# Row sums of a 16384 x 1024 matrix: two-part row ownership, an early store, and a last row in three pieces

## The chip, the cores and the metric

The kernel runs on one core of one Trainium2 chip. The metric is the device time of one execution in microseconds (us). A profile's *span* is about 1.8 us shorter than the time of the same execution (for the profiled execution of the kernel before: 164.42 us of time, 162.6 us of span). A *packet* is one piece of a transfer as the trace records it on one of the core's 16 DMA engines. A DMA has *landed* when the last of its completion signals (updates of a semaphore, a counter that instructions wait for) is recorded.

## The reference

```python
x = randn(32, 512, 1024) as float32          # 64 MiB
out = (np.sum(x, axis=-1) / 1024.0).astype(np.float32)     # (32, 512), 64 KiB
```

## The kernel before

Each of the 128 partitions (the rows of the on-chip memory) owns 128 consecutive rows, so its part of the input starts 512 KiB after its neighbour's, and its results are one run of 512 bytes of the output. Blocks of 14 rows come in through three buffers. VectorE sums some rows of a block in one instruction, and ScalarE sums the others one at a time, with the accumulator of its activation. The blocks get smaller towards the end, and the last row comes in two pieces. One store writes all results at the very end.

```python
xr = x.tensor.reshape((P, J, D)).ap()          # P = J = 128, D = 1024
out_v = out.tensor.reshape((P, J)).ap()
# ... (bulk: 8 loads of 14 rows, one of 8; tail: 4 rows, 2 rows)
c = 704
t = one.tile([P, D], F32, name="row")          # last row but one
tc.keep_in_program_order(nc.sync.dma_start(out=t, in_=xr[:, j, :]))
act_sum(part[:, 0:1], t[:, c:])
nc.vector.reduce_sum(out=part[:, 1:2], in_=t[:, :c], axis=AX)
nc.vector.tensor_scalar(out=res[:, j : j + 1], in0=part[:, 1:2], scalar1=part[:, 0:1],
                        scalar2=scale, op0=ADD, op1=MULT)
nc.vector.tensor_scalar_mul(out=res[:, :j], in0=res[:, :j], scalar1=scale)
j += 1
t = one.tile([P, D], F32, name="last")         # last row, two pieces
tc.keep_in_program_order(nc.sync.dma_start(out=t[:, :c], in_=xr[:, j, :c]))
tc.keep_in_program_order(nc.sync.dma_start(out=t[:, c:], in_=xr[:, j, c:]))
act_sum(part[:, 2:3], t[:, :c])
nc.vector.reduce_sum(out=part[:, 3:4], in_=t[:, c:], axis=AX)
nc.vector.tensor_scalar(out=res[:, j : j + 1], in0=part[:, 3:4], scalar1=part[:, 2:3],
                        scalar2=scale, op0=ADD, op1=MULT)
tc.keep_in_program_order(nc.sync.dma_start(out=out_v, in_=res))
```

## Time and profile before

| | before |
|---|---|
| time, median of 3 | 163.96 us (163.89 to 164.11) |
| span of the profiled execution | 162.6 us |
| last byte of the loads is in | 158.90 us |
| store issued | 160.22 us |
| packets of the store | 161.07 to 161.42 us |
| store landed | 161.77 us |
| 57,344-byte packets: median, mean, longest | 2116, 2138, 2967 ns |

The last load byte, the store's packets and the packet durations come from the trace's record of single DMA packets, and the landing from its record of completion signals. The other numbers are lines of the profile.

From the page of the kernel before: busy time by engine, the first line of the chain of waits that ended last, and the store's entry among the DMA issues (its last number is us from issue to landing).

```profile
DVE 79.3 (49%) x16; ACT 61.1 (38%) x115; POOL 0.2 (0%) x4
...
DMA 74%; DVE 18%; another core or an unknown queue 5%; SPq 1%; issue 0%; DVEq 0%
...
out_dram<-res SPq DMA_DIRECT2D x1, 64.0 KB, 1.5
```

No engine is busy even half of the time, and three quarters of the chain is DMA. Next, the same kernel by stretches of time; the last two columns are the share of the 16 DMA engines in use and the GB/s that they moved.

```profile
core 0: us, DVE busy (x) ACT busy (x) POOL busy (x), PEclk, DMA share, GB/s
50.00:100.00 50.00, 26.06 (x3) 19.03 (x36) 0.00 (x0) 1.00 0.99 426
100.00:144.00 44.00, 21.67 (x3) 16.92 (x33) 0.00 (x0) 1.00 1.00 433
...
160.00:162.60 2.60, 0.20 (x1) 0.00 (x0) 0.00 (x0) 1.00 0.09 25
```

The DMA engines are full until the loads end. A 57,344-byte packet in 2116 ns is 27.1 GB/s on one engine, or 434 GB/s for sixteen, and that is the speed seen. The engines have no idle time left in these stretches that a reordering could fill, and the median of 2116 ns is the same in the trace of every run of this case. So what follows the last load byte is what is left to shorten. (That nothing could make the packets themselves quicker is argued here, not shown.) The timeline of that end (start, duration, engine, line, operation, output and input):

```profile
start us, us, engine line op out<-in xcount [idle before <-releaser]
...
159.03 0.76 ACT L50 ACTIVATE junk<-last 128x704 f32<-128x704 f32 x1 [0.32 <-DMA last<-in_x_dram]
159.27 0.21 DVE L76 TENSOR_SCALAR res<-part 128x1 f32<-128x1 f32 x1
159.40 0.47 DVE L87 TENSOR_REDUCE part<-last 128x1 f32<-128x320 f32 x1
159.72 0.19 ACT L50 ACTIVATION_READ_ACCUMULATOR junk<-last 128x1 f32 x1
159.98 0.21 DVE L88 TENSOR_SCALAR res<-part 128x1 f32<-128x1 f32 x1
160.22 0.35 SPq L91 DMA_DIRECT2D out_dram<-res  x1
```

The last VectorE sum starts at 159.40, the combine at 159.98, the store's issue at 160.22. After the issue 2.4 us pass until the span ends at 162.65: the store itself and the end of the program. The waits of the queue that issues the DMAs show one delay that costs nothing, and the wait for the store that does:

```profile
engine line waited for: us in total, times, longest us
...
SPq L91 <- DMA t<-in_x_dram: 5.5, 1, 5.5
SPq L122 <- DMA out_dram<-res: 1.0, 1, 1.0
```

The first line is the store waiting for an earlier load, which is over long before its data are ready (L91 is the store). The second is the end of the program (L122) waiting for the store to land.

### The profile page before, as it was taken

What the parts mean: (1) busy time and instruction counts of PE and PEld (TensorE: products, weight loads), DVE (VectorE), ACT (ScalarE), POOL (GpSimd) and SP (SyncE); (2) the same over time, 40 slices, a digit from 0 to 9 for tenths busy, and PEclk for the clock granted to TensorE, in tenths of its full rate; (3) what the DMA queues carried; (4) which work ended last, traced back from release to release, by engine and by line L of the source; (5) the groups of instructions that cost most, each with busy time, mean ns of one, the idle gap of its engine ahead of it and who ended that gap; (6) DMA issues with size and microseconds to landing.
All of it is one profiled execution on the core that took longest, in us unless ns stands there. A gap on an engine that the chain in (4) does not pass through costs nothing.

```text
span 162.6 us, 213 instructions
## 1 busy us (share of the span) xinstructions
DVE 79.3 (49%) x16; ACT 61.1 (38%) x115; POOL 0.2 (0%) x4
## 2 busy tenths in 40 slices
DVE  0000099207940596039801990099108930697893
ACT  3000096006800490029201940095007700692882
POOL 0000000000000000000000000000000000000000
DMA  6999999989999999899999999999999999998990
GB/s 226 451 451 451 451 437 395 437 353 409 451 451 451 451 451 437 381 423 395 423 423 451 451 453 451 451 451 437 409 409 423 409 423 423 443 435 383 423 373 22
DMA packets 2161, 67.18 MB, mean 413 GB/s; under 512 B 240, under 2 KB 496, under 8 KB 752
## 3 DMA queue, kind: packets, MB, share of 16 engines
q1 hardware_dynamic: 2160, 67.18, 96.5%
q14 instruction: 1, 0.01, 0.0%
HBM read 67.11 MB, written 0.07 MB: 413 GB/s over the span
## 4 chain that ended last, share of the span: by engine, by line
DMA 74%; DVE 18%; another core or an unknown queue 5%; SPq 1%; issue 0%; DVEq 0%
DMA t<-in_x_dram 48%; DMA tail<-in_x_dram 25%; DVE res L56 17%; DVE part L75 0%; SPq L61 0%; SPq L66 0%; DVE part L87 0%; DVE res L79 0%; DVE res L88 0%; DVE res L76 0%; DVEq L88 0%; DVEq L76 0%; DVEq L79 0%
## 5 line engine op out<-in xcount | busy, mean ns | idle before, releaser
L56 DVE TENSOR_REDUCE res<-t 128x8 f32<-128x8192 f32 (+1 forms) x9 | 73.9, 8212 | 79.9 <-DMA t<-in_x_dram 79.9
L50 ACT ACTIVATE junk<-t 128x1024 f32<-128x1024 f32 x52 | 52.5, 1009 | 96.7 <-DMA t<-in_x_dram 96.7
L50 ACT ACTIVATION_READ_ACCUMULATOR junk<-t 128x1 f32 x52 | 9.7, 186 | 0.0
L56 DVE TENSOR_REDUCE res<-tail 128x2 f32<-128x2048 f32 (+1 forms) x2 | 3.5, 1753 | 0.7 <-DMA tail<-in_x_dram 0.7
L50 ACT ACTIVATE junk<-tail 128x1024 f32<-128x1024 f32 x3 | 3.1, 1022 | 0.9 <-DMA tail<-in_x_dram 0.9
L50 ACT ACT_TABLE_LOAD x1 | 1.3, 1283 | 0.7 <-PEq L108 0.7
L50 ACT ACTIVATE junk<-last 128x704 f32<-128x704 f32 x1 | 0.8, 761 | 0.3 <-DMA last<-in_x_dram 0.3
L75 DVE TENSOR_REDUCE part<-row 128x1 f32<-128x704 f32 x1 | 0.9, 880 | 0.0
L50 ACT ACTIVATION_READ_ACCUMULATOR junk<-tail 128x1 f32 x3 | 0.6, 186 | 0.0
L50 ACT ACTIVATE junk<-row 128x320 f32<-128x320 f32 x1 | 0.4, 441 | 0.1
L87 DVE TENSOR_REDUCE part<-last 128x1 f32<-128x320 f32 x1 | 0.5, 475 | 0.0
L79 DVE TENSOR_SCALAR res<-res 128x126 f32<-128x126 f32 x1 | 0.2, 228 | 0.1
L88 DVE TENSOR_SCALAR res<-part 128x1 f32<-128x1 f32 x1 | 0.2, 214 | 0.1
L76 DVE TENSOR_SCALAR res<-part 128x1 f32<-128x1 f32 x1 | 0.2, 214 | 0.1
L50 ACT ACTIVATION_READ_ACCUMULATOR junk<-last 128x1 f32 x1 | 0.2, 187 | 0.0
L50 ACT ACTIVATION_READ_ACCUMULATOR junk<-row 128x1 f32 x1 | 0.2, 186 | 0.0
L108 POOL MEMSET const-bfloat16-1.0<- 128x1 bf16 x1 | 0.1, 101 | 0.0
L108 POOL MEMSET const-uint8-127<- 128x1 uint8 x1 | 0.1, 101 | 0.0
L108 POOL MEMSET const-float32-0.0<- 128x1 f32 x1 | 0.1, 98 | 0.2 <-issue 0.2
L108 POOL MEMSET const-float32-1.0<- 128x1 f32 x1 | 0.1, 98 | 0.0
## 6 DMA issues: line engine op xcount, KB each, us to landing
t<-in_x_dram SPq DMA_DIRECT2D x8, 7168.0 KB, 42.1
t<-in_x_dram SPq DMA_DIRECT2D x1, 4096.0 KB, 34.8
tail<-in_x_dram SPq DMA_DIRECT2D x1, 2048.0 KB, 39.3
tail<-in_x_dram SPq DMA_DIRECT2D x1, 1024.0 KB, 41.4
row<-in_x_dram SPq DMA_DIRECT2D x1, 512.0 KB, 42.2
last<-in_x_dram SPq DMA_DIRECT2D x1, 352.0 KB, 42.6
last<-in_x_dram SPq DMA_DIRECT2D x1, 160.0 KB, 42.5
out_dram<-res SPq DMA_DIRECT2D x1, 64.0 KB, 1.5
```

Source lines behind the costliest of these rows:

```text
L50: nc.scalar.activation(junk[:, :n], src, COPY, accum_out=dst)
L56: nc.vector.reduce_sum(out=res[:, j : j + d], in_=t[:, :d, :], axis=AX)
L75: nc.vector.reduce_sum(out=part[:, 1:2], in_=t[:, :c], axis=AX)
L76: nc.vector.tensor_scalar(out=res[:, j : j + 1], in0=part[:, 1:2], scalar1=part[:, 0:1], scalar2=scale, op0=ADD, op1=MULT)
L79: nc.vector.tensor_scalar_mul(out=res[:, :j], in0=res[:, :j], scalar1=scale)
L87: nc.vector.reduce_sum(out=part[:, 3:4], in_=t[:, c:], axis=AX)
L88: nc.vector.tensor_scalar(out=res[:, j : j + 1], in0=part[:, 3:4], scalar1=part[:, 2:3], scalar2=scale, op0=ADD, op1=MULT)
L108: nc = _bacc.Bacc("TRN2", target_bir_lowering=False, num_devices=1)
```

## The change

The intent: nearly all results should leave while the end of the loads is being summed, so that the last store carries little, and the tail after the last load should be short. For this the rows are split in two parts. A partition owns 126 rows of the first part and 2 of the second. The store of the first part goes out as soon as it is summed and scaled. The last row comes in three pieces; the sums of the first two are written beside the third, so that one reduction of 258 columns finishes it. The multiply of the first part moves from VectorE to GpSimd.

```diff
-    xr = x.tensor.reshape((P, J, D)).ap()
-    out_v = out.tensor.reshape((P, J)).ap()
+    L = 2
+    M = J - L
+    x_main = bass.AP(tensor=x.tensor, offset=0, ap=[[M * D, P], [D, M], [1, D]])
+    x_last = bass.AP(tensor=x.tensor, offset=P * M * D, ap=[[L * D, P], [D, L], [1, D]])
+    o_main = bass.AP(tensor=out.tensor, offset=0, ap=[[M, P], [1, M]])
+    o_last = bass.AP(tensor=out.tensor, offset=P * M, ap=[[L, P], [1, L]])
 # ... (cut: the block loads keep their sizes; the row before the last is split at 768, not 704.
#      q and r hold two columns each: q takes VectorE's sums, r those of ScalarE, already scaled.
#      For the last row r is 0, because its ScalarE sum goes into pc)
-    tc.keep_in_program_order(nc.sync.dma_start(out=t[:, :c], in_=xr[:, j, :c]))
-    tc.keep_in_program_order(nc.sync.dma_start(out=t[:, c:], in_=xr[:, j, c:]))
-    act_sum(part[:, 2:3], t[:, :c])
-    nc.vector.reduce_sum(out=part[:, 3:4], in_=t[:, c:], axis=AX)
-    nc.vector.tensor_scalar(
-        out=res[:, j : j + 1], in0=part[:, 3:4], scalar1=part[:, 2:3], scalar2=scale, op0=ADD, op1=MULT
-    )
-    tc.keep_in_program_order(nc.sync.dma_start(out=out_v, in_=res))
+    a, b = 512, 768
+    pa = one.tile([P, a], F32, name="pa")
+    pb = one.tile([P, b - a], F32, name="pb")
+    pc = one.tile([P, D - b + 2], F32, name="pc")
+    load(pa, x_last[:, 1, :a])
+    load(pb, x_last[:, 1, a:b])
+    load(pc[:, : D - b], x_last[:, 1, b:])
+
+    nc.gpsimd.tensor_scalar_mul(out=res, in0=res, scalar1=scale)
+    tc.keep_in_program_order(nc.sync.dma_start(out=o_main, in_=res))
+
+    act_sum(pc[:, D - b : D - b + 1], pa)
+    nc.vector.reduce_sum(out=pc[:, D - b + 1 :], in_=pb, axis=AX)
+    nc.vector.reduce_sum(out=q[:, 1:2], in_=pc, axis=AX)
+    nc.vector.scalar_tensor_tensor(out=fin, in0=q, scalar=scale, in1=r, op0=MULT, op1=ADD)
+    tc.keep_in_program_order(nc.sync.dma_start(out=o_last, in_=fin))
```

More of the change, by code (lines that the diff above doesn't have):

```diff
@@ L29 @@
     assert J * P == N
-    xr = x.tensor.reshape((P, J, D)).ap()
-    out_v = out.tensor.reshape((P, J)).ap()
-    bulk = [14] * 7 + [14, 8]
+    L = 2
[4 more added lines that the diff above has]
+    o_last = bass.AP(tensor=out.tensor, offset=P * M, ap=[[L, P], [1, L]])
     split = {14: 6, 8: 4, 4: 2, 2: 1}
-    tail = [4, 2]
@@ L39 @@
-    assert sum(bulk) + sum(tail) + 2 == J
-    pool = ctx.enter_context(tc.tile_pool(name="bulk", bufs=3))
+    loads = [14] * 8 + [8, 4, 2]
+    assert sum(loads) == M
+    bulk = ctx.enter_context(tc.tile_pool(name="bulk", bufs=3))
     one = ctx.enter_context(tc.tile_pool(name="one", bufs=1))
     psum = ctx.enter_context(tc.tile_pool(name="junk", bufs=4, space=bass.MemoryType.PSUM))
-    res = one.tile([P, J], F32, name="res")
-    part = one.tile([P, 4], F32, name="part")
-    def act_sum(dst, src):
+    res = one.tile([P, M], F32, name="res")
@@ L48, in act_sum, with load @@
+    fin = one.tile([P, L], F32, name="fin")
+    q = one.tile([P, L], F32, name="q")
+    r = one.tile([P, L], F32, name="r")
+    nc.gpsimd.memset(r, 0.0)
+    def load(dst, src):
+        tc.keep_in_program_order(nc.sync.dma_start(out=dst, in_=src))
+    def act_sum(dst, src, by=1.0):
         n = src.shape[-1]
         junk = psum.tile([P, D], F32, name="junk")
-        nc.scalar.activation(junk[:, :n], src, COPY, accum_out=dst)
-    def sums(t, j, rows):
+        nc.scalar.activation(junk[:, :n], src, COPY, scale=by, accum_out=dst)
@@ L53, in sums @@
+    j = 0
+    for rows in loads:
+        if rows >= 8:
+            t = bulk.tile([P, 14, D], F32, name="t")
+        else:
+            t = one.tile([P, rows, D], F32, name=f"t{rows}")
+        load(t[:, :rows, :], x_main[:, j : j + rows, :])
         d = rows - split[rows]
-        for r in range(d, rows):
-            act_sum(res[:, j + r : j + r + 1], t[:, r, :])
+        for i in range(d, rows):
+            act_sum(res[:, j + i : j + i + 1], t[:, i, :])
         nc.vector.reduce_sum(out=res[:, j : j + d], in_=t[:, :d, :], axis=AX)
-    j = 0
@@ L59 @@
-    for i, rows in enumerate(bulk):
-        t = pool.tile([P, 14, D], F32, name="t")
-        tc.keep_in_program_order(nc.sync.dma_start(out=t[:, :rows, :], in_=xr[:, j : j + rows, :]))
-        sums(t, j, rows)
-        j += rows
-    for i, rows in enumerate(tail):
-        t = one.tile([P, rows, D], F32, name=f"tail{i}")
-        tc.keep_in_program_order(nc.sync.dma_start(out=t, in_=xr[:, j : j + rows, :]))
-        sums(t, j, rows)
-        j += rows
-    c = 704
-    t = one.tile([P, D], F32, name="row")
@@ L73 @@
-    tc.keep_in_program_order(nc.sync.dma_start(out=t, in_=xr[:, j, :]))
-    act_sum(part[:, 0:1], t[:, c:])
-    nc.vector.reduce_sum(out=part[:, 1:2], in_=t[:, :c], axis=AX)
-    nc.vector.tensor_scalar(
-        out=res[:, j : j + 1], in0=part[:, 1:2], scalar1=part[:, 0:1], scalar2=scale, op0=ADD, op1=MULT
-    )
-    nc.vector.tensor_scalar_mul(out=res[:, :j], in0=res[:, :j], scalar1=scale)
-    j += 1
-    t = one.tile([P, D], F32, name="last")
-    tc.keep_in_program_order(nc.sync.dma_start(out=t[:, :c], in_=xr[:, j, :c]))
@@ L85 @@
-    tc.keep_in_program_order(nc.sync.dma_start(out=t[:, c:], in_=xr[:, j, c:]))
-    act_sum(part[:, 2:3], t[:, :c])
-    nc.vector.reduce_sum(out=part[:, 3:4], in_=t[:, c:], axis=AX)
-    nc.vector.tensor_scalar(
-        out=res[:, j : j + 1], in0=part[:, 3:4], scalar1=part[:, 2:3], scalar2=scale, op0=ADD, op1=MULT
-    )
-    tc.keep_in_program_order(nc.sync.dma_start(out=out_v, in_=res))
+        j += rows
+    c = 768
+    row = one.tile([P, D], F32, name="row")
+    load(row, x_last[:, 0, :])
@@ new lines @@
+    act_sum(r[:, 0:1], row[:, c:], by=scale)
+    nc.vector.reduce_sum(out=q[:, 0:1], in_=row[:, :c], axis=AX)
+    a, b = 512, 768
[7 more added lines that the diff above has]
+    tc.keep_in_program_order(nc.sync.dma_start(out=o_main, in_=res))
```

## The prediction

> **What bounds it now.** The loads. In the windows view DMA share is 0.99 to 1.01 and 426 to 433 GB/s in every long stretch from 8 to 144 us; VectorE is busy 49% and ScalarE 38% of the span (page, part 1). The packet records show 16 packets in flight almost all the time. The usual 57,344-byte packet takes 2116 ns (median), 27.1 GB/s on one engine, so the 16 engines run at about 434 GB/s: a limit per engine that a reordering cannot lift. The mean is 2138 ns, because some packets near the start (up to 2967 ns) and up to about 70 us are slower. At median speed throughout, 64 such packets per engine would save at most 64 x 22 ns = 1.4 us.
>
> **The tail now.** Last load packet ends at 158.9; landing is seen about 0.5 us later (row: packets end 157.6, ScalarE starts 158.15). Timeline: VectorE reduces 320 columns 159.40 to 159.87, combines 159.98 to 160.19, the store is issued 160.22, its packets run 161.07 to 161.43, it lands 161.7, and the span ends 162.6. So 3.7 us follow the last load byte, of which 0.8 us is arithmetic and about 2.4 us is store issue, landing and program end.
>
> **What changes.**
> 1. Tail arithmetic. The last row is 512+256+256 instead of 704+320. ScalarE on 512 columns: about 0.72 us with its read (from 0.69 us for 704 issued to done and 0.37 for 320: I estimate 0.53+0.19 at worst). It can start near 158.75, done 159.45. VectorE: row reduce on 768 columns, 0.95 us by 1.05 ns a column, 158.1 to 159.05; 256-column piece, 0.41 us, to about 159.5; then third piece with both sums, 258 columns, 0.41 us, from about 159.55 to 160.0; combine 160.1 to 160.3. Store issue near 160.3: no earlier than before, because one dependent VectorE step (0.1 us gap each) and the serial pieces replace what was saved.
> 2. The final store shrinks from 128 x 512 bytes to 128 x 8. Packets of 512 took 27 ns, 4-byte ones 9 ns: about 0.15 us less moving; the fixed path (0.85 us issue to first packet, 0.3 to landing, 0.9 to end) stays. The Trainium skill, "DMA: Bandwidth & Descriptors", section Specifications, says transfers below 512 B are read-modify-write; both stores now are (504 and 8 B). No trace here shows the price; I allow 0 to 0.3 us.
> 3. The 126-column multiply goes to GpSimd (0.23 us on VectorE today); main store issued about 158.7, after the last load's issue, packets after 159.4, landed by 160.5: hidden.
> 4. Row pitch of the big loads becomes 504 KiB instead of 512 KiB. The same page, section "Latency and other measured facts", measures 207 GB/s at 512 KiB against 214 padded. Here the slow packets could be that; they cost at most 1.4 us plus end skew. I expect about 0.6 us back.
> 5. One more load issue: hidden; it waits for a transfer eight earlier (about 5.5 us, as the store does today).
>
> **Critical path.** Loads minus 0.6, tail 0 +/- 0.3: predicted 163.3 us, range 162.3 to 164.3. Faster by over 2%: 3%; within 2%: 94%; slower by over 2%: 3%.
>
> **What shows it.** Large-packet mean nearer 2116 ns; last load byte near 158.3; final store issued 1.4 us after the last load byte (1.3 now); main store landed before the final store is issued; issue to landing of the final store 1.3 to 1.6 us.
>
> **What would make it wrong.** The new pitch aliasing worse or much better; small writes costing over 0.5 us; ScalarE's write beside the third piece waiting for that piece's landing (+0.7 us); GpSimd's multiply taking over 1.5 us, so the main store lands last.

## The result, and the profile after

The changed kernel took 165.76 us (165.48 to 166.05, 4 runs) beside 164.04 us (163.89 to 164.28, 4 runs) for the kernel before. The ratio is 1.0104, with a 95% interval of 1.0082 to 1.0126: about 1.7 us slower, clear of the noise, and outside the predicted range of 162.3 to 164.3. A ratio is the mean time of one kernel's fast runs over that of the other's in the same rounds, so it is not quite the ratio of the medians.

| profiled executions | before | after |
|---|---|---|
| span | 162.65 | 163.71 us |
| last load byte | 158.90 | 158.63 us |
| last store issued (after the last load byte) | 160.22 (+1.32) | 160.03 (+1.40) us |
| packets of the last store end | 161.42 | 161.06 us |
| last store, issue to landing | 1.5 | 2.7 us |
| last store issued to end of the span | 2.43 | 3.68 us |
| 57,344-byte packets: mean, longest | 2138, 2967 | 2129, 3286 ns |

The two profiled executions are 1.06 us apart and the medians 1.72: the profiled execution of after was the fastest of its four (165.48), and that of before was slower than its median (164.42). So the traces show the kind of the loss, and less than its whole size.

The page, the DMA issues and the stretches of the changed kernel:

```profile
DVE 79.4 (48%) x15; ACT 60.9 (37%) x115; POOL 0.8 (1%) x6
...
DMA 74%; DVE 16%; another core or an unknown queue 5%; SPq 1%; issue 0%; ACT 0%; ACTq 0%; DVEq 0%
```

```profile
out_dram<-res SPq DMA_DIRECT2D x1, 63.0 KB, 2.0
out_dram<-fin SPq DMA_DIRECT2D x1, 1.0 KB, 2.7
```

```profile
core 0: us, DVE busy (x) ACT busy (x) POOL busy (x), PEclk, DMA share, GB/s
50.00:100.00 50.00, 26.06 (x3) 19.03 (x36) 0.00 (x0) 1.00 1.00 433
100.00:144.00 44.00, 22.02 (x3) 17.27 (x33) 0.00 (x0) 1.00 0.99 427
...
160.00:163.70 3.70, 0.00 (x1) 0.00 (x0) 0.00 (x0) 1.00 0.02 0
```

The load speed and the engines' busy times are nearly as before. What differs is in the DMA issues: the last store carries 1 KB, not 64, and takes 2.7 us to land, not 1.5. In the last stretch nearly nothing is busy. The end of the timeline:

```profile
start us, us, engine line op out<-in xcount [idle before <-releaser]
...
157.88 0.54 POOL L92 TENSOR_SCALAR res<-res 128x126 f32<-128x126 f32 x1 [157.07 <-DVE res L71]
...
158.44 0.35 SPq L93 DMA_DIRECT2D out_dram<-res  x1
158.54 0.60 ACT L59 ACTIVATE junk<-pa 128x512 f32<-128x512 f32 x1 [0.16 <-DMA pa<-in_x_dram]
158.80 0.42 DVE L96 TENSOR_REDUCE pc<-pb 128x1 f32<-128x256 f32 x1
159.08 0.19 ACT L59 ACTIVATION_READ_ACCUMULATOR junk<-pa 128x1 f32 x1
159.31 0.42 DVE L97 TENSOR_REDUCE q<-pc 128x1 f32<-128x258 f32 x1
159.84 0.16 DVE L98 SCALAR_TENSOR_TENSOR fin<-q,r 128x2 f32<-128x2 f32 x1
160.03 0.34 SPq L99 DMA_DIRECT2D out_dram<-fin  x1
```

The last store is issued at 160.03, 0.19 us earlier than before, and then nothing is left but to wait for it. The waits of the issuing queue say the same (L93 is the early store, L54 the loads, L130 the end of the program; the waits for earlier loads are over long before the data of the early store are ready, and cost nothing):

```profile
engine line waited for: us in total, times, longest us
...
SPq L93 <- DMA t<-in_x_dram: 16.6, 1, 16.6
SPq L54 <- DMA t<-in_x_dram: 5.4, 1, 5.4
SPq L130 <- DMA out_dram<-fin: 2.3, 1, 2.3
```

The end of the program waits 2.3 us for the last store, against 1.0 before. The packet records add where in the store the time lies: its packets are over at 161.06 us, earlier than those of the store before (161.42), and the landing is seen at 162.77. The bytes have left quickly; the confirmation comes 1.7 us later, against 0.35 before (161.42 to 161.77). The trace has 16 completion signals for each store. Before, they come between 161.59 and 161.77 us; here the first comes at 161.28 and the last at 162.77, spread over 1.5 us. So the parts of this store are not all late by the same time: they are confirmed one after another. The Trainium skill, "DMA: Bandwidth & Descriptors", section "Anatomy of one DMA", says of a DMA's fixed cost (on the GpSimd path) that the semaphore update cannot fire until the last byte is confirmed landed in the target memory. This trace, on the Sync path, agrees in kind: the 1.7 us lie between the last packet and the semaphore.

### The profile page after: what moved, and what is told of

Same layout as the page of the kernel before. It is cut to its first block, busy times and chain, and to the rows that moved or that the text cites. A ratio compares the mean times of both kernels' runs of the same rounds, so it can differ in the third digit from the quotient of the medians.

```text
span 163.7 us, 220 instructions
## 1 busy us (share of the span) xinstructions
DVE 79.4 (48%) x15; ACT 60.9 (37%) x115; POOL 0.8 (1%) x6
## 4 chain that ended last, share of the span: by engine, by line
DMA 74%; DVE 16%; another core or an unknown queue 5%; SPq 1%; issue 0%; ACT 0%; ACTq 0%; DVEq 0%
DMA t<-in_x_dram 48%; DMA pa<-in_x_dram 26%; DVE res L71 16%; SPq L54 1%; ACT junk L59 0%; DVE q L97 0%; DVE fin L98 0%; ACTq L130 0%; DVEq L98 0%; ACTq L59 0%
## 5 line engine op out<-in xcount | busy, mean ns | idle before, releaser
L71 DVE TENSOR_REDUCE res<-t 128x8 f32<-128x8192 f32 (+3 forms) x11 | 77.4, 7038 | 80.3 <-DMA t<-in_x_dram 80.3
L59 ACT ACTIVATE junk<-t 128x1024 f32<-128x1024 f32 x55 | 55.5, 1009 | 97.3 <-DMA t<-in_x_dram 97.3
L59 ACT ACTIVATION_READ_ACCUMULATOR junk<-t 128x1 f32 x55 | 10.2, 186 | 0.0
L92 POOL TENSOR_SCALAR res<-res 128x126 f32<-128x126 f32 x1 | 0.5, 536 | 157.1 <-DVE res L71 157.1
L79 DVE TENSOR_REDUCE q<-row 128x1 f32<-128x768 f32 x1 | 1.0, 952 | 0.1
L59 ACT ACTIVATE junk<-pa 128x512 f32<-128x512 f32 x1 | 0.6, 601 | 0.2 <-DMA pa<-in_x_dram 0.2
```

What stands on the lines that cost most here:

```text
L59: nc.scalar.activation(junk[:, :n], src, COPY, scale=by, accum_out=dst)
L71: nc.vector.reduce_sum(out=res[:, j : j + d], in_=t[:, :d, :], axis=AX)
L79: nc.vector.reduce_sum(out=q[:, 0:1], in_=row[:, :c], axis=AX)
L92: nc.gpsimd.tensor_scalar_mul(out=res, in0=res, scalar1=scale)
```

## The experiments

The question was what makes a store of 1 KB land later than one of 64 KB. Theories: A1, a run of 8 bytes is slow by itself; A2, runs side by side in a small stretch of memory hold each other up; B, the last store is held up behind the early store; C, the loss, or part of it, is in the new layout of the loads or in the tail. Kernels of one group ran on one chip and shared its runs of the kernel before.

### No early store

```diff
-    tc.keep_in_program_order(nc.sync.dma_start(out=o_main, in_=res))
```

Wrong (most outputs stay unwritten).

> The changed kernel without its early store (most outputs stay unwritten, wrong on purpose). In the changed kernel the last store of 128 x 8 bytes took 2.7 us from issue to landing, the store before took 1.5. Theory A (runs of 8 bytes are slow to complete by themselves): the last store still takes 2.5 to 2.8 us, the time stays within 0.3 us of the changed kernel's 165.8. Theory B (the last store is held up behind the early store in the same rings): it falls to about 1.4 us and the time to about 164.5.

Measured: 165.64 us, ratio 1.0088 (1.0069 to 1.0107). The DMA issue of its last store:

```profile
out_dram<-fin SPq DMA_DIRECT2D x1, 1.0 KB, 3.3
```

The last store is at least as slow with nothing ahead of it (3.3 us is even above the 2.5 to 2.8 that I had written), so B falls. That the early store is on the critical path falls too: without it the time stays.

### One late store of 512-byte runs, all else as changed

```diff
-    res = one.tile([P, M], F32, name="res")
-    fin = one.tile([P, L], F32, name="fin")
+    res = one.tile([P, J], F32, name="res")
+    fin = res[:, M:]
@@ ...
-    tc.keep_in_program_order(nc.sync.dma_start(out=o_main, in_=res))
@@ ...
-    tc.keep_in_program_order(nc.sync.dma_start(out=o_last, in_=fin))
+    tc.keep_in_program_order(nc.sync.dma_start(out=out.tensor.reshape((P, J)).ap(), in_=res))
```

Wrong on purpose (values in displaced places).

> The changed kernel with both stores replaced by one late store of 128 x 512 bytes (values land in displaced places, wrong on purpose). Theories A and B both: issue to landing back at about 1.5 us, so 1.2 us less than the changed kernel: about 164.5 us. If the whole loss is the store and not the loads or the tail, the ratio to before is 1.000 to 1.002; a third theory (C, the loads of the new layout or the tail's arithmetic cost some tenths) gives 1.003 or more.

Measured: 164.15 us, ratio 0.9998 (0.9984 to 1.0013). Its store:

```profile
out_dram<-res SPq DMA_DIRECT2D x1, 64.0 KB, 1.5
```

The whole loss goes when the two stores go, with the new layout, the three pieces and the GpSimd multiply kept. C falls as a cause of the loss. I had written "about 164.5" beside the ratio; I took 1.2 us, the difference in one pair of traces, from the median, and the loss was larger than that.

### The kernel before with the store split in its own layout

```diff
+    K = J - 2
+    fin = one.tile([P, 2], F32, name="fin")
@@ ... (the combines of the last two rows write fin[:, 0:1] and fin[:, 1:2])
+    tc.keep_in_program_order(nc.sync.dma_start(out=out_v[:, :K], in_=res[:, :K]))
     act_sum(part[:, 2:3], t[:, :c])
@@ ...
-    tc.keep_in_program_order(nc.sync.dma_start(out=out_v, in_=res))
+    tc.keep_in_program_order(nc.sync.dma_start(out=out_v[:, K:], in_=fin))
```

> The kernel before with its store split into an early one of 128 x 504 bytes and a late one of 128 x 8 bytes, in its own output layout, where each run of 8 bytes lies 512 bytes from the next. Theory A1 (a short run is slow whatever its neighbours are): late store 2.5 to 2.8 us, time about 165.1. Theory A2 (the 8-byte runs of all partitions fall into two 512-byte blocks, and writes into one block wait for each other): late store 1.4 to 1.6 us, time about 163.9. Correct results.

Measured: correct, 163.94 us, ratio 0.9984 (0.9967 to 1.0001). The two stores, early one first:

```profile
out_dram<-res SPq DMA_DIRECT2D x1, 63.0 KB, 1.5
out_dram<-fin SPq DMA_DIRECT2D x1, 1.0 KB, 1.4
```

The same 128 runs of 8 bytes land in 1.4 us when they lie 512 bytes apart. A1 falls: the shortness of a run costs nothing here. Whether the small gain is real was left to a second timing (below).

### The new row layout alone

```diff
-    xr = x.tensor.reshape((P, J, D)).ap()
+    M = J - 2
+    x_main = bass.AP(tensor=x.tensor, offset=0, ap=[[M * D, P], [D, M], [1, D]])
+    x_last = bass.AP(tensor=x.tensor, offset=P * M * D, ap=[[2 * D, P], [D, 2], [1, D]])
@@ ... (loads from x_main and x_last; everything else as before)
```

Wrong on purpose (values in displaced places).

> The kernel before with the loads' row layout of the change (126 rows of a first part, 2 of a second; values displaced, wrong on purpose), everything else as before. My prediction expected about 0.6 us less (ratio 0.996). If the new layout costs time in the loads (theory C), ratio above 1.001. If layout is without effect, 0.999 to 1.001. Mean of the 57,344-byte packets 2129 ns as in the changed kernel's trace, against 2138.

Measured: 164.19 us, ratio 0.9999 (0.9985 to 1.0013); mean of the large packets 2130 ns. The layout neither costs nor gains anything that the timing resolves. The 0.6 us that I had predicted from it are not there: that gain would be a ratio of 0.996, below the interval. The packet records do show an effect, though a small one. From 10 to 80 us of the span, the large packets took longer than their median by 0.20 to 0.72 us per DMA engine, added up, in the four traces with the old layout of the loads (the kernel before, the split store twice, and the changed kernel in the old layout, below), and by 0.02 to 0.03 us in all nine traces with another. In the first 10 us the new layout changes nothing clear: 0.42 to 0.72 us in the old, 0.61 to 0.76 in the others.

### The changed kernel with its last store spread out

```diff
-    o_last = bass.AP(tensor=out.tensor, offset=P * M, ap=[[L, P], [1, L]])
+    scratch = nc.dram_tensor("scratch", (P * J,), F32, kind="Internal")
+    o_last = bass.AP(tensor=scratch, offset=M, ap=[[J, P], [1, L]])
```

Wrong (the last 256 outputs stay unwritten).

> The changed kernel with one thing altered: its last store of 128 runs of 8 bytes writes them 512 bytes apart into a scratch tensor (the last 256 outputs stay unwritten, wrong on purpose) and not side by side. Theory A2 (runs side by side in the same small stretch of memory wait for each other): last store 1.4 us from issue to landing against 2.7, time about 164.0, ratio to before 0.998 to 1.001. A rival, D (the split in 512_pitch was quick for another reason, such as the memory being recently written by the early store, or the layout of the loads): 2.5 to 3.3 us and about 165.7.

Measured: 164.04 us, ratio 0.9987 (0.9974 to 1.0000). Its stores, early one first:

```profile
out_dram<-res SPq DMA_DIRECT2D x1, 63.0 KB, 1.9
scratch<-fin SPq DMA_DIRECT2D x1, 1.0 KB, 1.4
```

Only the addresses of the last store are altered, no byte more or less is moved, and the loss is gone. From issue to end of the span it falls from 3.68 us to 2.32, and the 16 completion signals come within 0.16 us of each other. The addresses also lie in another tensor, but that is not the reason: in the ladder below, the crowded shape is slow in such a scratch tensor too (2.6 to 2.8 us). A2 holds.

### The changed kernel in the old output layout, and the split store again

The first kernel is the changed one with the rows owned as before:

```diff
-    x_main = bass.AP(tensor=x.tensor, offset=0, ap=[[M * D, P], [D, M], [1, D]])
-    x_last = bass.AP(tensor=x.tensor, offset=P * M * D, ap=[[L * D, P], [D, L], [1, D]])
-    o_main = bass.AP(tensor=out.tensor, offset=0, ap=[[M, P], [1, M]])
-    o_last = bass.AP(tensor=out.tensor, offset=P * M, ap=[[L, P], [1, L]])
+    xr = x.tensor.reshape((P, J, D)).ap()
+    out_v = out.tensor.reshape((P, J)).ap()
+    x_main = xr[:, :M, :]
+    x_last = xr[:, M:, :]
+    o_main = out_v[:, :M]
+    o_last = out_v[:, M:]
```

> The changed kernel whole (early store, three pieces, GpSimd multiply), but with the rows owned as before, 128 in a row per partition, so that the early store is 504 bytes at 512 and the last one 8 bytes at 512. Correct. Theory A2: last store 1.4 us, early store 1.5 us (2.0 in the changed kernel), time about 163.9, ratio 0.998 to 1.000. If the changed layout's own loss were elsewhere, this would still be at 1.003 or more.

Measured: correct, 164.41 us, ratio 1.0008 (0.9995 to 1.0021). Its stores:

```profile
out_dram<-res SPq DMA_DIRECT2D x1, 63.0 KB, 1.5
out_dram<-fin SPq DMA_DIRECT2D x1, 1.0 KB, 1.4
```

The loss is gone here as well, though the ratio came out just above the range that I had written. The second kernel is the one of the split store, unedited, timed with more rounds:

> The same kernel as split_512_pitch, timed again with five rounds because it came out 0.9984 with an interval that touches 1. If the early store is worth the 0.15 us that the bytes of the last store cost (eight packets of 27 ns against eight of about 9 ns per engine), ratio 0.998 to 0.9995; if worth nothing, 0.9995 to 1.0005.

Measured: 164.00 us, ratio 0.9985 (0.9968 to 1.0001). Two timings on two chips agree on 0.15%, but each interval touches 1. Why the first kernel is some 0.2% behind the second, in the same rounds and with equally quick stores, was not settled. The trace of the first has the last load byte at 158.92 us, that of the second at 158.71, and three pieces put 1.40 us between that byte and the issue against 1.25; single traces differ by that much for other reasons too.

### A ladder of stores

```python
# behind the last store of the changed kernel; each store waits for the one before,
# because the memset of s does
scratch = nc.dram_tensor("scratch", (P * 256 * 48,), F32, kind="Internal")
s = one.tile([P, 256], F32, name="s")
def to(k, pitch, width):
    nc.vector.memset(s, 1.0)
    return bass.AP(tensor=scratch, offset=k * P * 256, ap=[[pitch, P], [1, width]])
for k in (0, 15, 30):  # 8 B at 8
    d = to(k, 2, 2)
    tc.keep_in_program_order(nc.sync.dma_start(out=d, in_=s[:, :2]))
# ... and so on for 15 shapes, three stores each, after one store that is not counted
```

> The changed kernel followed by a ladder of stores into scratch memory, one at a time, three of each shape (time meaningless, outputs correct). Theory A2 with a block of B bytes: 8-byte runs at a pitch of 8 take 2.5 to 3.3 us, falling in steps as the pitch grows through 16, 32, 64, 128, 256 and reaching about 1.4 at the pitch where every run has a block of its own; contiguous runs of 32, 64, 128, 256 bytes get quick once a run fills a block. Theory A1 (short run alone) is already against split_512_pitch and would need all 8-byte shapes alike. 504 at 504 should take about 2.0 as in the changed kernel, 504 at 512 and 512 at 512 about 1.5.

Measured, us from issue to landing (outputs correct; one execution):

| 128 runs of | laid out every | each of three |
|---|---|---|
| 8 B | 8 B | 2.72, 2.63, 2.84 |
| 8 B | 16 B | 1.38, 1.39, 2.16 |
| 8 B | 32, 64, 128, 256, 512 B | 1.38 to 1.42 (15 stores) |
| 32 B | 32 B | 2.07, 1.39, 1.38 |
| 64 B, 128 B | the same | 1.39 to 1.42 (6 stores) |
| 256 B | 256 B | 1.44, 1.43, 1.47 |
| 504 B | 504 B | 1.65, 2.11, 1.65 |
| 504 B | 512 B | 1.51, 1.51, 1.52 |
| 512 B | 512 B | 1.51, 1.54, 1.51 |
| 1024 B | 1024 B | 1.66, 1.66, 1.66 |

A2 was right that neighbours matter, and I had the size of the neighbourhood wrong: I had written of blocks of 512 bytes, but 16 runs to a 512-byte block (8 B every 32) already land in 1.39 us. The crowding has to be closer than that. Two more rows deserve a look. The single 2.07 us among the 32-byte runs is probably no crowding: a packet of 8192 bytes that the trace marks as fetching instructions ran during that store, and during none of the other 44. And wide runs are not free by their width: runs of 504 bytes side by side took 1.65 to 2.11 us, the same 504 bytes every 512 took 1.51. (I had written 2.0 for the first; one of three came near.) The early stores fit: 1.9 to 2.0 us side by side, 1.5 in the old layout. Why runs of 504 bytes pay and runs of 24 bytes, in the next ladder, hardly do, was not settled.

### A finer ladder

Same form, six stores of each shape, each starting on a multiple of 8192 bytes from the start of the scratch tensor. The last shape lays the runs so that neighbours in memory are 8 partitions apart:

```python
for k in range(60, 66):
    d = to(k, [2, 16], [32, 8], [1, 2])     # partition 8u+v goes to place u + 16v
```

> A second ladder of single stores behind the changed kernel, six of each shape (time meaningless, outputs correct). The first ladder showed 8 bytes side by side at 2.63 to 2.84 us, 8 bytes every 16 at 1.38, 1.39 and 2.16, and 8 bytes every 32 or more, or 32-byte runs side by side, at about 1.39. Theory S (a chain: writes into one small unit follow each other, each waiting for the one before): 4 bytes side by side are slower than 8, 3.5 us or more; 12 and 16 side by side lie between 1.4 and 2.7. Theory T (a step: only runs under some size side by side pay, once): 4 and 8 alike at 2.7. Of the two last shapes, the second lays runs that are 8 partitions apart side by side: if neighbours must come from one engine to collide, it takes 1.4; if any neighbours collide, 2.6 or more; the first of the two is the plain order in the same form and should take 2.7.

Measured (outputs correct; one execution; min, median, max of six, us):

| 128 runs of | laid out every | min / median / max |
|---|---|---|
| 4 B | 4 B | 6.9 / 7.6 / 7.9 |
| 8 B | 8 B | 2.8 / 3.7 / 3.8 |
| 12 B | 12 B | 2.0 / 2.6 / 2.7 |
| 16 B | 16 B | 1.4 / 1.6 / 2.1 |
| 24 B | 24 B | 1.4 / 1.4 / 1.5 |
| 32 B | 32 B | 1.4 / 1.4 / 1.4 |
| 8 B | 16 B | 1.4 / 1.9 / 2.5 |
| 8 B | 24 B | 1.4 / 1.6 / 2.0 |
| 8 B | 32 B | 1.4 / 1.4 / 1.7 |
| 8 B | 8 B, written as 16 x 8 | 2.8 / 3.0 / 3.1 |
| 8 B | 8 B, neighbours 8 partitions apart | 3.2 / 3.3 / 3.4 |

The first row, as the profile gives it for the line of that store:

```profile
L112 SPq DMA_DIRECT2D scratch<-s x6: 319/320/327, 163.9 to 203.7; - x6
...
DMA to landing us min/median/max: 6.9/7.6/7.9
```

The 4-byte runs, 512 bytes in all, take five times as long as the 32-byte runs, 4 KB. It is all confirmation: the packets of the 4-byte stores, too, are over 1.0 us after the issue. (The same shape varies as well: 8 bytes side by side took 2.6 to 2.8 us in the first ladder and 2.8 to 3.8 here, and 8 bytes every 16 took 1.4 us in the first two stores of six and 2.2 to 2.5 in the last three. The reason is open.) The cost grows with the number of runs per stretch of memory: against the 1.4 us of uncrowded stores, runs every 12 bytes add 1.2 us, every 8 bytes 2.3, every 4 bytes 6.2 (medians). This is theory S as far as its growth goes: a chain would give it, and a single step would not. The completion signals fit a chain: in the first 4-byte store they come one by one from 2.8 to 6.9 us after the issue. What the unit of memory is, and that it is a chain inside it, are not shown: I only argue it from the growth and the spread. S in the form that neighbours must come from one place gets no support: neighbours 8 partitions apart are as slow. (Their issue takes 0.2 us longer and their packets end some 0.35 us later than in the plain order, 1.37 to 1.47 us after the issue and not 1.02; from the last packet to landing both take about 1.9 us.) Which DMA engine serves which partition is not in the trace, so whether two engines or one collide stays open.

### Wider runs in the changed kernel

The second part gets 8 rows per partition, so that the runs of the last store are 32 bytes.

```diff
-    L = 2
+    L = 8
-    loads = [14] * 8 + [8, 4, 2]
+    loads = [14] * 8 + [8]
@@ ... (the loads of 4 and 2 rows now come from x_last; ScalarE's sums go to r, scaled,
@@      VectorE's to q, which starts at zero, and the final combine makes fin = q * scale + r
@@      for all 8 columns)
```

> The changed kernel with 120 rows per partition in the first part and 8 in the second, so that the last store is 32-byte runs side by side; early store, three pieces and GpSimd multiply kept. Correct. By the ladder the last store lands in 1.4 us: time about 164.0, ratio to before 0.998 to 1.0005. If the loss of the changed kernel had to do with its two-part layout and not with the width of the runs, about 165.7.

Measured: correct, 163.81 us, ratio 0.9981 (0.9968 to 0.9994), last store 1.4 us. The loss is gone when the last store is not crowded. Then the same with the last row in two pieces:

```diff
-    a, b = 512, 768        # three pieces
-    act_sum(pc[:, D - b : D - b + 1], pa)
-    nc.vector.reduce_sum(out=pc[:, D - b + 1 :], in_=pb, axis=AX)
-    nc.vector.reduce_sum(out=q[:, E + 1 :], in_=pc, axis=AX)
+    a = 704                # two pieces; E = L - 2
+    act_sum(r[:, E + 1 :], last[:, :a], by=scale)
+    nc.vector.reduce_sum(out=q[:, E + 1 :], in_=last[:, a:], axis=AX)
```

> As eight_rows, with the last row in two pieces (704 and 320 columns) as in the kernel before, and one VectorE sum and one combine after the last load. The traces so far give 1.32 us from the last load byte to the issue of the last store with two pieces and 1.40 with three; here one vector step is shorter, so about 1.25. Expected ratio 0.997 to 0.9985, the best of all, about 163.8 us; if three pieces are no worse, it equals eight_rows.

Measured: correct, 163.69 us, ratio 0.9976 (0.9962 to 0.9989), the fastest of all. Its stores:

```profile
out_dram<-res SPq DMA_DIRECT2D x1, 60.0 KB, 5.0
out_dram<-fin SPq DMA_DIRECT2D x1, 4.0 KB, 1.4
```

The early store is issued at 154.03 us, 5.0 us before it lands; its packets run from 157.5 to 158.6 us, around the last load byte at 158.39, so it sits behind nearly all of the loads and is over before the last store is issued. Last load byte to issue is 1.28 us (1.34 with three pieces), and issue to end of the span 2.25 us (2.43 in the kernel before). The two kernels' intervals overlap, so the worth of two pieces over three is not shown. Both intervals lie below 1: both beat the kernel before, by 0.2%. How much of that the early store earns is not shown: issue to end of the span is 0.2 us shorter in the traces, but the last load byte also comes 0.5 us earlier (158.39 and 158.34 against 158.90), and the layout of the loads is another one here. The changed kernel's own interval (1.0082 to 1.0126, in other rounds) lies well above.

## Why the prediction was wrong

- *What bounds it*: right as far as it was measured. The loads run at 426 to 433 GB/s in both kernels, and the early part of the chain is unchanged.
- *1, tail arithmetic*: right. I gave 1.4 us from the last load byte to the last issue, against 1.3; the traces show 1.40 and 1.32. Three pieces and one more dependent VectorE step buy nothing.
- *2, the final store*: this is the step that failed. I wrote that it saves "about 0.15 us" of moving, that the fixed path "stays", with "0.3 to landing", and for writes below 512 bytes "I allow 0 to 0.3 us". The packets did end sooner (161.06 against 161.42 us). But issue to landing was 2.7 us in the trace of the changed kernel and 3.3 in that without the early store, where I had written 1.3 to 1.6. Set against the 1.4 us of the spread store, that is 1.3 to 1.9 us, and the timed loss is 1.7. The list of what could go wrong names "small writes costing over 0.5 us", so the mechanism was in view; but I took it to be a matter of size. The runs show that it is not: 8-byte runs 512 bytes apart land in 1.4 us, sooner than 512-byte runs in 1.5. It is crowding. With only that store spread out, the changed kernel took 164.04 us, inside the range (164.28 for the kernel before on that chip).
- *3, GpSimd multiply and early store hidden*: right. The multiply took 0.54 us (0.23 on VectorE before). The early store landed at 158.44 + 2.0 = 160.4, after the last store's issue and not before it as I had said, without consequence: without it the ratio stays at 1.0088.
- *4, row pitch*: too large. I expected 0.6 us; alone the layout gave 0.9999 (0.9985 to 1.0013). I had put two kinds of slow packets down to the pitch. Those of the first 10 us did not go: the longest is 3286 ns in the new layout and 2967 in the old. Those up to about 70 us did: 0.20 to 0.72 us per engine in the four traces with the old layout, 0.03 or less in the others. So half of the idea held, but the time did not follow to any amount that the timing resolves. The 207 and 214 GB/s that I had cited were measured on other transfers than these loads (copies between HBM tensors), and its 214 on a padded pitch of 4 MiB.
- *5, one more load issue*: right. The profile lists a wait of 5.4 us at the load lines, and it is hidden.

## What to carry to other kernels

Judge a small last store by how closely its runs crowd in memory, not by its bytes: choose the ownership of rows so that each partition's run keeps some distance to the next, or is itself not tiny. In these runs 32 bytes were enough, as a run or as the distance from one start to the next (1.4 us in the median). Runs of 504 bytes side by side still paid 0.1 to 0.6 us, so measure the shape that you choose. Before moving work out of a last step, ask what part of the step scales with its size; here the bytes were worth some 0.15 us of 2.4 (packets over 0.19 us and not 0.35). And read issue to landing, not the packets, when a program ends on a store.

## What the Trainium skill lacked or had wrong

- "DMA: Bandwidth & Descriptors", Specifications, gives 512 bytes as the least transfer for line rate and read-modify-write below it. It does not say when a small store lands, and applied to that it led this prediction to look at the size of a run: with 32 bytes or more from one to the next, runs of 8 bytes land in 1.4 us (median; 1.7 at most) and 512-byte runs in 1.5. The page lacks what did cost here: runs of 4, 8 and 12 bytes side by side, 7.6, 3.7 and 2.6 us (medians of six) against 1.4 for runs of 24 and 32 bytes.
- The same page, "Latency and other measured facts", has 207 GB/s at a row pitch of 512 KiB, and 214 for a padded pitch of 4 MiB, for copies between HBM tensors. It does not cover loads into the on-chip memory (SBUF). For these, 504 KiB in place of 512 took 0.2 to 0.7 us of slow packets away per engine, but gave a ratio of 0.9999 (0.9985 to 1.0013), so no gain of that size.
- No page that I read has the time from issue to landing of a small store from the Sync queue by its shape; here it is 1.4 us for 1 to 16 KB, 1.5 for 64 KB and 1.7 for 128 KB, uncrowded.
